# RWKV-7 chunk scan in a hybrid attention layer: the prompt as a third lane beside the sample's two directions, Gram products on quarters of the array

## The chip, the cores and the metric

The kernel runs on one core of one Trainium2 chip. The metric is the device time of one execution in microseconds (us), lower is better. The engines named below are PE (TensorE, matrix products), DVE (VectorE), ACT (ScalarE), POOL (GpSimd) and SP, the queue that issues every DMA of this kernel.

## The reference

One layer of a hybrid backbone is computed for 512 sample tokens and 128 prompt tokens (width 2048). A shared input projection feeds eight attention heads and sixteen RWKV-7 heads of 64; their outputs are joined, projected, normalised, and followed by a SwiGLU feed-forward part. What the change touches is the RWKV scan: for each of 16 heads a 64x64 state S is carried along the tokens, once forward and once backward. The sample's scans start from given states, the prompt's scans start from zero, and the prompt's final states are outputs.

```python
def step(S, inp):
    r_t, w_t, k_t, v_t, kk_t, a_t = inp
    sa = jnp.einsum("bhvk,bhk->bhv", S, -kk_t)
    S = S * w_t[:, :, None, :] + sa[..., None] * (kk_t * a_t)[:, :, None, :] + v_t[..., None] * k_t[:, :, None, :]
    return S, jnp.einsum("bhvk,bhk->bhv", S, r_t)
...
for w0, w_up, a0, a_up, s0, rev in directions:
    s_fin, y_dir = _wkv_scan(s0, r_h, heads(decay), k_dir, v_h, kk, heads(a), rev)
    ys.append(y_dir)
y = ys[0] + ys[1]
```

## The kernel before

The tokens lie along the free axis, 640 columns (512 sample, then 128 prompt); features lie on the 128 partitions. The program has two stages. In the first, several jobs share PE: the input projection (`main`), the modulation weights (`wmods`), the RWKV scan (`rwkv`) and, when `main` has ended, the attention (`attention`). Each job is a generator that yields the time for which it expects to wait; a planner (`Jobs`) keeps a model of PE's time (`Tensor.now`), always takes the ready job of lowest rank (RWKV is rank 0, the projection 4, the attention 3) and so writes down one fixed order of PE's instructions. The waits it reckons with are constants in a table (`HOP`). The other engines' queues are ordered by the framework's scheduler. The second stage (output projection and feed-forward part, tile names `b`, `qh`, `mx`) begins when the first has ended and is not touched.

The scan is worked in chunks of 64 tokens, ten chunks for 640 tokens, for two heads at a time (a pair, one head on each half of the partitions): 8 pairs, each in two passes j = 0, 1. In a pass the columns are two halves of 320: half j is walked forward (d = 0), the other half backward (d = 1, its columns reversed by `view`). So each pass has two lanes of five chunks, chunk e of lane d being number 5d + e; a second pass continues from the carried states `cy`. The prompt's two chunks stand at the end of the forward order, and its states start from zero inside the lane (table `AFTER`).

A pass goes like this:
- `rwkv_decays` and `rwkv_prep` make `nk` (two key-like factors of 64 rows per head) and `pr` (two query-like factors).
- `rwkv_grams` forms for each chunk and head h the 128x128 Gram product of `nk` and `pr`: stationary `nk` with 64 rows and 128 columns, moving `pr` with 128 columns, so one half of the array's rows per head; the heads go to two PSUM banks. Four chunks fill the banks; ACT copies out `mab` and `mrb`, DVE masks the rest into `pr`. At the end DVE masks `mrb` in one go.
- `inverse` inverts the triangular `mab` (DVE, and packed 32x32 products on PE). Beside it run `rwkv_turned` (turns the values `v` into `sv` and `zv` and `nk` into `bk`, on PE) and a side job: `beside_first` (normalisation and gate of the pair before, `rwkv_post`, then the decays of the second pass) or `beside_second` (bonus term, then the next pair's load and decays).
- `rwkv_chain` walks the five steps. A step is: px = pr x sv (4 products), copied to `xs` by ACT; the products of the outputs of the step before (`outputs`, 8 products in two banks); psg = u x xs (4), copied to `zv` by ACT (head 0) and DVE (head 1); pn = bk x zv (4), and four scalar_tensor_tensor on DVE that write the next state into `sv`. POOL prepares the decayed state `sd`. After psg and after pn the planner may put other jobs' work.

PSUM tiles of the RWKV part are named `m` (three banks); those of the projection `acc`; of the modulation weights and the attention's values `x`. All matrix work of the projection and the scores uses the whole 128x128 array. Helper lines: L115 matmul, L119 transpose, L229 tensor_tensor, L238 scalar_tensor_tensor, L241 activation; L878 copies `xs`, L899 and L900 copy `zv`, L816 and L820 copy `mab` and `mrb`, L956 stores the pair's result, L1245 stores an attention head, L847 loads the states, L448 stores the shifted r, k, v.

Of the kernel before, what the change touches and what calls it, by code (L numbers as in the profile page):

```python
# [11 lines left out]
ALU = mybir.AluOpType  # L12
# [3 lines left out]
P = 128  # L16
# [30 lines left out]
for _n, _w in (("ident", 128), ("gmask", 128), ("lmask", 32), ("par", 2), ("blk", 128), ("cen", 128), ("blk2", 2), ("sel", 2),  # L47
               ("ones", 1), ("rst", 320), ("rot", 128)):
    CST[_n] = (_off, _w)
    _off += _w  # L50
# [110 lines left out]
def step_kernel(ctx: ExitStack, tc: tile.TileContext, a: dict, o: dict, upto: int = 99, npairs: int = NPAIR, dbg=None):  # L161
# [32 lines left out]

    def half(name):
        return rtile(name, HN, "h", 1)
# [210 lines left out]
    def token_shift(p0, p1, mi, mk=edge):  # L407
# [12 lines left out]
        return ((slice(0, NS), s[:, :NS]), (slice(NS, NT), s[:, 513:641]))  # L420
# [260 lines left out]
    def nat(d, j):  # L681

        h = j if d == 0 else 1 - j
        return slice(h * HN, h * HN + HN)

    def view(t, d, j):
        v = t[:, nat(d, j)]
        return v if d == 0 else v[:, ::-1]
# [25 lines left out]
    HV = [slice(0, HN), slice(HN, NT)]  # L714

    def rwkv_decays(i, j, sh):
# [3 lines left out]
        for d in range(2):  # L720
# [3 lines left out]
            for t, w, x, r_, b, ps in both:  # L724
                T.matmul(ps[:, :HN], w, x[:, nat(d, j)], start=True, stop=False)

            for t, w, x, r_, b, ps in both:
                T.matmul(ps[:, :HN], w[r_], xl[r_, nat(d, j)], start=False, stop=True, share=0.5)
            for t, w, x, r_, b, ps in both:
                od = t[:, HV[d]] if d == 0 else t[:, HV[d]][:, ::-1]  # L730
                act(od, ps[:, :HN], AF.Tanh, bias=b[:, col: col + 1], scale=0.5)
            yield 2 * HOP["dec"]
        ts(V, ld, ld, -0.5 * EXPH, -0.5 * EXPH)
        for v_ in HV:
            V.tensor_tensor_scan(out=ld[:, v_], data0=con("rst"), data1=ld[:, v_], initial=0.0, op0=ALU.mult, op1=ALU.add)
# [6 lines left out]
        for d in range(2):  # L742
            stt(nb[:, HV[d]], ta[:, HV[d]], 1.0, view(kk, d, j), ALU.add, ALU.mult)
        ts(V, ta, ta, ka_h[:, i: i + 1], ka_c[:, i: i + 1])
        for d in range(2):
            tt(V, ta[:, HV[d]], ta[:, HV[d]], view(k, d, j), ALU.mult)
        for d in range(2):
            n_ = ks[:, nat(d, j)]
            src = ta[:, HV[d]] if d == 0 else ta[:, HV[d]][:, ::-1]
# [6 lines left out]
    def rwkv_prep(i, j, sh, u):  # L756
# [5 lines left out]
        for h in range(2):  # L762
# [3 lines left out]
            for d in range(2):  # L766
                es = slice(5 * d, 5 * d + 5)
                kv_, rv_ = (ch(t[rh, nat(d, j)]) for t in (kk, r))
                if d == 1:
# [3 lines left out]
                tt(G, pr[h][rh, es, 1, :], rv_, dd5[rh, es, :], ALU.mult)  # L773
        yield HOP["prep"] + (FIRST[1] if i + j == 0 else 0.0)

    def rwkv_turned(i, j, sh, u):

        nk, v = u["nk"], sh["v"]
# [1288 lines left out]
```

## Time and profile before

| | |
|---|---|
| runs (3) | median 3418.34 us, 3415.4 to 3426.62 |
| profiled execution | 3418.1 us, its instructions span 3416.3 us |
| first stage | 0 to 1434 us |
| RWKV passes | first chain about 260 us, last result stored at 1428.9 us |
| attention heads stored | 1155.1 to 1433.0 us |
| mean granted PE clock | 0.969 |

A row of the profile names the engine, the operation, the tile written and the tiles read, then the shape. PE writes two records for a float32 product and one for a product of rounded operands. In a row of PE, `64*128` is the part of the array in use (rows*columns). A burst of equal products is merged into one row of the timeline with its count; the time from its start to the next row's start is what it takes of PE's time, since records overlap.

### The profile page before, as it was taken

What the parts mean: (1) busy time and instruction counts of PE and PEld (TensorE: products, weight loads), DVE (VectorE), ACT (ScalarE), POOL (GpSimd) and SP (SyncE); (2) the same over time, 40 slices, a digit from 0 to 9 for tenths busy, and PEclk for the clock granted to TensorE, in tenths of its full rate; (3) what the DMA queues carried; (4) which work ended last, traced back from release to release, by engine and by line L of the source; (5) the groups of instructions that cost most, each with busy time, mean ns of one, the idle gap of its engine ahead of it and who ended that gap; (6) DMA issues with size and microseconds to landing.
All of it is one profiled execution on the core that took longest, in us unless ns stands there. A gap on an engine that the chain in (4) does not pass through costs nothing.

```text
span 3416.3 us, 71056 instructions
## 1 busy us (share of the span) xinstructions
PE 3231.4 (95%) x27746; PEld 2973.9 (87%) x27746; DVE 2489.4 (73%) x4469; ACT 1447.3 (42%) x3028; POOL 994.2 (29%) x1034
## 2 busy tenths in 40 slices
PE   7999998999997988899989999999999999999998
PEld 3777777777876777799989999999999999999997
DVE  2466675666658666568688888888887769999677
ACT  1344343444444545445454444444444444333234
POOL 0012222222222222112265444444442332222124
PEclk9999998999998999999989999999999999999998
DMA  9755454542222110275434443344444367888643
GB/s 359 241 185 166 145 171 142 158 151 94 66 63 84 44 34 28 79 246 173 145 108 154 149 139 124 127 141 135 130 123 121 114 218 278 298 286 285 214 142 119
DMA packets 289344, 527.71 MB, mean 154 GB/s; under 512 B 30512, under 2 KB 76272, under 8 KB 289008
## 3 DMA queue, kind: packets, MB, share of 16 engines
q1 hardware_dynamic: 289008, 523.18, 46.7%
q8 instruction: 217, 3.56, 0.4%
q14 instruction: 119, 0.97, 0.1%
HBM read 428.99 MB, written 92.44 MB: 153 GB/s over the span
## 4 chain that ended last, share of the span: by engine, by line
PE 65%; DVE 8%; ACT 3%; issue 2%; DMA 2%; POOL 2%; SPq 0%; ACTq 0%; DVEq 0%; POOLq 0%
PE b L115 51%; PE acc L115 7%; PE m L115 5%; PE x L115 1%; DVE ql L229 1%; DVE pr L229 1%; POOL z L229 1%; DVE z L229 1%; DVE ip L229 1%; ACT z L241 0%; DMA z<-zd 0%; PE acc L119 0%; DMA k<-rkv 0%; DVE nk L238 0%; DVE wlo L229 0%
## 5 line engine op out<-in xcount | busy, mean ns | idle before, releaser
L229 DVE TENSOR_TENSOR ql<-raw,qh 128x512 fp32r<-128x512 f32 (+1 forms) x1064 | 888.6, 850 | 264.9 <-ACT qh L1307 250.6
L1307 ACT CAST qh<-raw 128x512 fp32r<-128x512 f32 (+1 forms) x1064 | 633.5, 610 | 831.0 <-PE b L115 643.2
L115 PE MATMUL b<-t,qh 128*128 128x320 f32 x2816 | 623.4, 310 | 8.3 <-ACT qh L1307 7.1
L229 POOL TENSOR_TENSOR raw<-raw,raw 128x512 f32<-128x512 f32 x240 | 351.8, 1466 | 807.1 <-DVE ql L229 561.2
L115 PE MATMUL b<-op,qh 128*128 128x320 f32 x2560 | 552.8, 311 | 2.0 <-DMA op<-hd 1.2
L115 PEld LDWEIGHTS b<-t,qh 128*128 128x128 f32 x2816 | 473.1, 189 | 9.6 <-ACT qh L1307 8.1
L115 PE MATMUL b<-p,qh 128*128 128x320 f32 x2112 | 469.5, 311 | 0.0
L115 PE MATMUL b<-t,ql 128*128 128x320 f32 x1408 | 436.2, 311 | 5.4 <-DVE ql L229 5.4
L115 PEld LDWEIGHTS b<-op,qh 128*128 128x128 f32 x2560 | 425.8, 189 | 4.0 <-ACT qh L1307 1.9
L115 PE MATMUL b<-op,ql 128*128 128x320 f32 x1280 | 378.9, 311 | 5.6 <-DVE ql L229 5.5
L115 PEld LDWEIGHTS b<-p,qh 128*128 128x128 f32 x2112 | 356.9, 190 | 0.1
L115 PE MATMUL b<-p,ql 128*128 128x320 f32 x1056 | 329.4, 312 | 6.1 <-DVE ql L229 6.1
L115 PE MATMUL acc<-xh,whi 128*128 128x320 f32 x1056 | 265.2, 333 | 9.7 <-ACT P L1170 3.9
L115 PEld LDWEIGHTS b<-t,ql 128*128 128x128 f32 x1408 | 265.3, 189 | 7.3 <-DVE ql L229 7.3
L115 PE MATMUL acc<-xh,wlo 128*128 128x320 f32 x1056 | 264.6, 333 | 4.8 <-DVE wlo L229 4.8
L115 PE MATMUL acc<-xl,whi 128*128 128x320 f32 x1056 | 261.5, 330 | 0.5 <-DVE xl L229 0.5
L115 PEld LDWEIGHTS b<-op,ql 128*128 128x128 f32 x1280 | 236.7, 189 | 8.4 <-DVE ql L229 8.2
L115 PE MATMUL b<-mh,qh 128*128 128x320 f32 x1024 | 230.2, 314 | 7.0 <-ACT qh L1307 6.0
L115 PEld LDWEIGHTS acc<-xh,whi 128*128 128x128 f32 x1056 | 180.8, 197 | 33.5 <-issue 12.7
L115 PEld LDWEIGHTS b<-p,ql 128*128 128x128 f32 x1056 | 200.1, 190 | 8.5 <-DVE ql L229 8.5
L229 DVE TENSOR_TENSOR wlo<-raw,whi 128x512 fp32r<-128x512 f32 (+1 forms) x161 | 110.3, 686 | 124.0 <-ACT whi L266 115.4
L115 PEld LDWEIGHTS acc<-xh,wlo 128*128 128x128 f32 x1056 | 180.6, 196 | 22.6 <-issue 9.2
(330 smaller groups left out, 5465.1 us busy)
## 6 DMA issues: line engine op xcount, KB each, us to landing
wm<-in_w_mod_dram SPq DMA_DIRECT2D x64, 1024.0 KB, 5.4
raw<-in_w_gate_dram SPq DMA_DIRECT2D x188, 256.0 KB, 2.7
raw<-in_w_up_dram SPq DMA_DIRECT2D x188, 256.0 KB, 2.9
op<-hd SPq DMA_DIRECT2D x136, 320.0 KB, 5.3
wm<-in_w_mod_dram SPq DMA_DIRECT2D x64, 512.0 KB, 7.5
raw<-in_w_out_dram SPq DMA_DIRECT2D x128, 256.0 KB, 2.9
raw<-in_w_down_dram SPq DMA_DIRECT2D x128, 256.0 KB, 5.4
raw<-in_w_in_dram SPq DMA_DIRECT2D x127, 256.0 KB, 2.7
```

The costliest lines, as they stand in the source:

```text
L115: self.eng.matmul(out, lhsT, rhs, start=start, stop=stop)
L229: eng.tensor_tensor(out=out, in0=x, in1=y, op=op)
L1307: A.copy(hi, x)
```

## The change

The columns of the RWKV part are kept in another order: 256 of the sample, the 128 of the prompt, the other 256 of the sample. A pass now has a segment of six chunks (columns 0 to 384) and one of four. In pass j the segment g is walked forward where g = j, backward otherwise. The six-chunk segment holds a lane of four chunks and, as a third lane, the prompt's two chunks, whose states start from zero at once. So a chain has four steps: two of three lanes and two of two lanes, ten chunks in all as before. The products of `outputs` for all lanes go to one PSUM bank instead of two.

The Gram product of a chunk and head is split into two products of 64 columns of `nk` each, four per chunk, each on its own quarter (64x64) of the array; the quarters that give `mab` and `mrb` of both heads now share one bank, so ACT copies `mab` for both heads at once, and DVE masks `mrb` straight out of PSUM, per group of four chunks. The turned values (`sv`, `zv`), until now made by `rwkv_turned`, are made inside `rwkv_grams`, after the second and the third group of chunks; the reversed copy `vr` is made at the end of `rwkv_prep`. `rwkv_turned` sets the start states (until now done by the chain) and makes `bk`. The shifted columns are stored with three DMAs instead of two, the pair's result with three instead of one. The decays' products are 384 and 256 columns wide instead of 320 and 320. A scratch area for DMAs is set to 1024 bytes; no constant of `HOP` is changed.

```diff
-        return ((slice(0, NS), s[:, :NS]), (slice(NS, NT), s[:, 513:641]))
+        return ((slice(0, 256), s[:, :256]), (slice(256, 384), s[:, 513:641]), (slice(384, NT), s[:, 256:NS]))
...
+    SEG = (slice(0, 384), slice(384, NT))
+    CHS = (slice(0, 6), slice(6, NCH))
...
     def rwkv_turned(i, j, sh, u):
-        nk, v = u["nk"], sh["v"]
-        vr = half("vr")
-        A.copy(vr, view(v, 1, j))
-        sv_, zv, bk = u["sv"], u["zv"], u["bk"] = wide("sv"), wide("zv"), wide("bk")
-        yield HOP["vr"]
-        for d in range(2):
-            src = v[:, nat(0, j)] if d == 0 else vr
-            es = slice(5 * d, 5 * d + 5)
-            ps = mps()
-            for c in range(5):
-                for h in range(2):
-                    T.matmul(ps[hrow(h), cc(c)], src[rows(h), cc(c)], ident[rows(h), rows(h)], start=True, stop=True)
-            for h in range(2):
-                A.copy(sv_[hrow(h), es, h, :], ch(ps[hrow(h), :HN]))
-                A.copy(zv[hrow(h), es, h, :], ch(ps[hrow(h), :HN]))
-            yield HOP["tv"]
+        nk, cy = u["nk"], sh["carry"]
+        sv_, bk = u["sv"], u["bk"]
+        for h in range(2):
+            if j == 0:
+                for d, q in ((0, 0), (1, 6)):
+                    DMA.dma_start(out=sv_[rows(h), q, h, :], in_=a["states"][d, i, rows(h)])
+                G.memset(sv_[rows(h), 4, h, :], 0.0)
+            else:
+                G.tensor_copy(sv_[rows(h), 2:7:4, h, :], cy[rows(h)].rearrange("p (d v) -> p d v", v=C))
+                G.memset(sv_[rows(h), 0, h, :], 0.0)
+        yield 0.4
...
-        for e0, n in EG:
+        for n_, (e0, n) in enumerate(EG):
             es = slice(e0, e0 + n)
             both = [mps(), mps()]
             for e in range(n):
-                for h, ps in enumerate(both):
-                    T.matmul(ps[:, e * P: e * P + P], nk[rows(h), e0 + e].rearrange("p b t -> p (b t)"),
-                             pr[h][rows(h), e0 + e].rearrange("p b t -> p (b t)"), start=True, stop=True, share=0.5)
-            for h, ps in enumerate(both):
-                ps4 = ps[:, :n * P].rearrange("p (c b t) -> p c b t", b=2, t=C)
-                q = 1 - h
-                A.copy(mab[rows(h), es], ps4[rows(h), :, 0, :])
-                tt(V, pr[h][rows(q), es].rearrange("p c b t -> p c (b t)"),
-                   ps4[rows(q)].rearrange("p c b t -> p c (b t)"),
-                   con("gmask")[rows(q)].unsqueeze(1).broadcast_to([C, n, P]), ALU.mult)
-                A.copy(mrb[rows(h), es], ps4[rows(h), :, 1, :])
+                for h in range(2):
+                    for b in range(2):
+                        T.matmul(both[b != h][rows(b), e * P: e * P + P], nk[rows(h), e0 + e, b, :],
+                                 pr[h][rows(h), e0 + e].rearrange("p b t -> p (b t)"), start=True, stop=True, share=0.33)
+            pa, pb = (ps[:, :n * P].rearrange("p (c b t) -> p c b t", b=2, t=C) for ps in both)
+            A.copy(mab[:, es], pa[:, :, 0, :])
+            for h in range(2):
+                q = rows(1 - h)
+                tt(V, pr[h][q, es].rearrange("p c b t -> p c (b t)"), pb[q].rearrange("p c b t -> p c (b t)"),
+                   con("gmask")[q].unsqueeze(1).broadcast_to([C, n, P]), ALU.mult)
+            tt(V, mrb[:, es], pa[:, :, 1, :], con("gmask")[:, C:].unsqueeze(1).broadcast_to([P, n, C]), ALU.mult)
+            if n_:
+                values(n_ - 1)
             yield 2 * HOP["gram"]
-        tt(V, mrb, mrb, con("gmask")[:, C:].unsqueeze(1).broadcast_to([P, NCH, C]), ALU.mult)
...
-        for e in range(5):
+        for e in range(4):
+            qs_ = lanes(e)
             px = mps()
-            for d in range(2):
+            for l, q in enumerate(qs_):
                 for h in range(2):
-                    T.matmul(px[rows(h), cc(d)], pr[h][:, 5 * d + e, 0, :], sv_[:, 5 * d + e, h, :], start=True, stop=True)
+                    T.matmul(px[rows(h), cc(l)], pr[h][:, q, 0, :], sv_[:, q, h, :], start=True, stop=True)
...
-            A.copy(lanes(zv, 0, e), lane2(psg, 0))
-            V.tensor_copy(lanes(zv, 1, e), lane2(psg, 1))
+            A.copy(both(zv, 0, e), lane2(psg, 0))
+            V.tensor_copy(both(zv, 1, e), lane2(psg, 1))
+            if len(qs_) > 2:
+                A.copy(zv[rows(0), qs_[2], 0, :], psg[rows(0), cc(2)])
+                V.tensor_copy(zv[rows(1), qs_[2], 1, :], psg[rows(1), cc(2)])
             yield HOP["s"]
...
-                for d in ds:
-                    q = 5 * d + e
...
-                    stt(dst, pn[rh, cc(d)], dc[rh, q: q + 1], sd[rh, cc(d)], ALU.mult, ALU.add)
+                for l in ls:
+                    dst = place(l, e)
+                    dst = dst[rh, h, :] if len(dst.shape) > 2 else dst[rh]
+                    stt(dst, pn[rh, cc(l)], dc[rh, qs_[l]: qs_[l] + 1], sd[rh, cc(l)], ALU.mult, ALU.add)
...
-        DMA.dma_start(out=mix_d[8 + i], in_=y)
+        for out, src in ((slice(0, 256), slice(0, 256)), (slice(256, NS), slice(384, NT)), (slice(NS, NT), slice(256, 384))):
+            DMA.dma_start(out=mix_d[8 + i][:, out], in_=y[:, src])
```

How PE's order changes is shown at two places. The first is the chain in the first pass of the third pair (`sv`, `pr`, `zv`, `bk`, `mrb`, `uf` are the chain's tiles, `acc` the projection's): a step of the chain before,

```order
L115 MATMUL m_6363<-xs_6346,uf_162 64x64 x4
L115 MATMUL acc_6070<-xh_922,wlo_6168 128x320 x2
L115 MATMUL acc_6070<-xh_931,whi_6167 128x320 x2
L115 MATMUL acc_6070<-xl_932,whi_6167 128x320 x2
L115 MATMUL acc_6070<-xh_931,wlo_6168 128x320 x2
L115 MATMUL m_6378<-zv_5778,bk_5779 64x64 x4
L115 MATMUL acc_6070<-xh_1184,whi_6266 128x320 x2
L115 MATMUL acc_6070<-xl_1185,whi_6266 128x320 x2
L115 MATMUL acc_6070<-xh_1184,wlo_6267 128x320 x2
L115 MATMUL m_6399<-sv_5777,pr_5542 64x64
```

and a step of three lanes in the changed kernel:

```order
L115 MATMUL m_6316<-xs_6293,uf_162 64x64 x6
L115 MATMUL acc_6163<-xl_634,whi_6164 128x320 x2
L115 MATMUL acc_6163<-xh_633,wlo_6165 128x320 x2
L115 MATMUL acc_6163<-xh_642,whi_6164 128x320 x2
L115 MATMUL acc_6163<-xl_643,whi_6164 128x320 x2
L115 MATMUL m_6335<-zv_5591,bk_5592 64x64 x6
L115 MATMUL acc_6163<-xh_642,wlo_6165 128x320 x2
L115 MATMUL acc_6163<-xh_651,whi_6164 128x320 x2
L115 MATMUL acc_6163<-xl_652,whi_6164 128x320 x2
L115 MATMUL m_6354<-sv_5590,pr_5556 64x64
```

The same amount of the projection's work stands between the bursts of a step; the bursts are longer, and a chain has four steps of them instead of five.

The second place is the turning of the values (`v`, `vr` against the identity in `cst`) in the next pass, the second of that pair. Before, the two bursts stand by themselves after the Gram products (`ks` and `wm` belong to other jobs):

```order
L115 MATMUL m_6710<-ks_5020,cst 128x320
L115 MATMUL m_6713<-cst,v_4911 64x64 x10
L115 MATMUL x_6611<-wm_1111_6612,cs 32x512 x4
L115 MATMUL m_6749<-cst,vr_6689 64x64 x10
L115 MATMUL acc_6524<-xl_932,whi_6577 128x320 x2
```

In the changed kernel each follows a group of Gram products (`pr`, `nk`; here the third and last group):

```order
L115 MATMUL m_6645<-pr_6471,nk_6470 64x128
L115 MATMUL m_6646<-pr_6471,nk_6470 64x128
L115 MATMUL m_6646<-pr_6472,nk_6470 64x128
L115 MATMUL m_6645<-pr_6472,nk_6470 64x128
L115 MATMUL m_6645<-pr_6471,nk_6470 64x128
L115 MATMUL m_6646<-pr_6471,nk_6470 64x128
L115 MATMUL m_6646<-pr_6472,nk_6470 64x128
L115 MATMUL m_6645<-pr_6472,nk_6470 64x128
L115 MATMUL m_6659<-cst,v_4960 64x64 x8
L115 MATMUL acc_6626<-xh_422,whi_6536 128x320 x2
```

The transposes of `v` and `vr` have moved into the Gram bursts, ahead of the inverse. On ACT the group's evictions, before this row set (one of the three groups),

```order
L816 COPY mab_6490<-m_6551 64x256
L816 COPY mab_6490<-m_6552 64x256
L266 CAST whi_6577<-raw_6529 128x512
L820 COPY mrb_6491<-m_6551 64x256
L820 COPY mrb_6491<-m_6552 64x256
```

become one copy followed by those of the values:

```order
L820 COPY mab_6512<-m_6564 128x256
L808 COPY sv_6509<-m_6586 64x6x64
L809 COPY zv_6510<-m_6586 64x6x64
L808 COPY sv_6509<-m_6586 64x6x64
L809 COPY zv_6510<-m_6586 64x6x64
```

Three of ACT's four copies of a group are gone from its queue; the values' copies, which stood behind the inverse's start, now stand ahead of it.

On DVE, the second step of a chain, with three lanes (a later pair; `y` the outputs, `zv` and `sv` as above, `fs` the prompt's final state) look like this; before, a step has one copy of `zv` and four scalar_tensor_tensor:

```order
L226 TENSOR_TENSOR y_9858<-m_10859,y_9858 128x64 x3
L913 COPY zv_10155<-m_10875 64x2x64
L916 COPY zv_10155<-m_10875 64x64
L235 SCALAR_TENSOR_TENSOR sv_10154<-m_10894,dc_9745,sd_10854 64x64 x2
L235 SCALAR_TENSOR_TENSOR fs_9857<-m_10894,dc_9745,sd_10854 64x64
L235 SCALAR_TENSOR_TENSOR sv_10154<-m_10894,dc_9745,sd_10854 64x64 x2
L235 SCALAR_TENSOR_TENSOR fs_9857<-m_10894,dc_9745,sd_10854 64x64
```

A three-lane step has six of these updates and two copies where a step before had four and one.

More of the change, by code (lines that the diff above doesn't have):

```diff
@@ L841, in rwkv_chain @@
+        gap = first[1] - first[0]
         if j == 0:
@@ L843, in rwkv_chain @@
             sh["y"] = slot("y")
-        for h in range(2):
-            if j == 0:
-                for d, e in ((0, 0), (1, 7)):
-                    DMA.dma_start(out=sv_[rows(h), e, h, :], in_=a["states"][d, i, rows(h)])
-                G.memset(sv_[rows(h), 5, h, :], 0.0)
-            else:
-                G.tensor_copy(lanes(sv_, h, 0), lane2(cy, h))
-                G.memset(sv_[rows(h), 3, h, :], 0.0)
-        y = sh["y"]
-        def outputs(c):
-            pss = [mps()[:, :C] for _ in range(2)]
-            ms = (slice(0, C), slice(None, None, -1))
-            for d, ps in enumerate(pss):
+        y, fs = sh["y"], sh["fs"]
@@ new lines, in lanes, with both, lane2, place @@
+        def lanes(e):
+            return [q + e for q in first] + ([(4, 0)[j] + e] if e < 2 else [])
+        def both(t, h, e):
+            return t[rows(h), first[0] + e: first[1] + e + 1: gap, h, :]
+        def lane2(t, h):
+            return t[rows(h), :2 * C].rearrange("p (d v) -> p d v", v=C)
+        def place(l, e):
+            if l == 2:
+                return sv_[:, lanes(e)[2] + 1] if e == 0 else fs[:, cc(j)]
+            if e < 3:
+                return sv_[:, lanes(e)[l] + 1]
+            return cy[:, cc(1 - l)] if j == 0 else None
@@ L860, in outputs @@
+        def outputs(e):
+            qs_ = lanes(e)
+            ps = mps()
+            turned = [(q >= 6) != j for q in qs_]
+            for l, q in enumerate(qs_):
                 for h in range(2):
-                    T.matmul(ps[rows(h)], sv_[:, 5 * d + c, h, :], pr[h][:, 5 * d + c, 1, :][:, ms[d]], start=True, stop=False)
-            for d, ps in enumerate(pss):
+                    T.matmul(ps[rows(h), cc(l)], sv_[:, q, h, :], pr[h][:, q, 1, :][:, ::-1 if turned[l] else 1],
+                             start=l == 0, stop=False)
+            for l, q in enumerate(qs_):
@@ L863, in outputs @@
                 for h in range(2):
-                    T.matmul(ps[rows(h)], zv[rows(h), 5 * d + c, h, :], mrb[rows(h), 5 * d + c, :][:, ms[d]], start=False, stop=True)
-            for d in range(2):
-                yc = y[:, nat(d, j)][:, cc(c if d == 0 else 4 - c)]
+                    T.matmul(ps[rows(h), cc(l)], zv[rows(h), q, h, :], mrb[rows(h), q, :][:, ::-1 if turned[l] else 1],
+                             start=False, stop=l == len(qs_) - 1)
+            for l, q in enumerate(qs_):
+                c = q if not turned[l] else 15 - q if q >= 6 else 5 - q
+                yc = y[:, cc(c)]
```

124 lines of the change are left out of this document (65 added, 59 removed).

## The prediction

> **What bounds the kernel now.** I read the page's busy shares first, then the table by stage, the waits of PE, and the timeline of PE inside one chain. The page:
>
> ```profile
> PE 3231.4 (95%) x27746; PEld 2973.9 (87%) x27746; DVE 2489.4 (73%) x4469; ACT 1447.3 (42%) x3028; POOL 994.2 (29%) x1034
> ```
>
> PE is nearly always busy. By stage (start, end and length in us, then busy time and count of PE, PEld, DVE, ACT and POOL, then the granted PE clock):
>
> ```profile
> 200.00:1060.00 860.00, 800.77 (x9820) 656.77 (x9819) 560.01 (x1230) 365.90 (x927) 190.53 (x324) 0.96 0.41 131
> 1060.00:1434.00 374.00, 328.26 (x3856) 285.60 (x3856) 251.92 (x581) 177.99 (x450) 93.75 (x141) 0.94 0.11 34
> ```
>
> The change lies in these 1234 us, of which PE is busy 1129; 105 us are idle. The clock costs more: 860 x 0.04 + 374 x 0.06 = 57 us. The two belong together:
>
> ```profile
> 936.00:939.00 3.00, 0.95 (x15) 0.96 (x14) 2.02 (x4) 0.00 (x0) 2.83 (x5) 1.00 0.55 151
> 939.50:942.90 3.40, 3.40 (x15) 3.40 (x14) 2.80 (x4) 1.65 (x4) 0.00 (x0) 0.50 0.27 96
> ```
>
> A gap of 2 us is followed by 3.4 us at half clock, so it costs nearly 4. Who is waited for (idle us, times, longest):
>
> ```profile
> PE m L115 <- DVE y L229: 22.1, 19, 2.7
> PE m L115 <- DVE zv L900: 6.5, 4, 4.1
> PE m L115 <- POOL sv L851: 6.0, 6, 1.2
> PE x L115 <- DMA wm<-in_w_mod_dram: 1.1, 1, 1.1
> ```
>
> No single wait is large, and hardly any is on a DMA. RWKV and attention, which fill PE together, end together (the stores of their results; min/median/max duration in ns, first and last start):
>
> ```profile
> L956 SPq DMA_DIRECT2D mix<-y x8: 319/326/327, 389.4 to 1428.9; - x8
> L1245 SPq DMA_DIRECT2D mix<-att x8: 320/326/327, 1155.1 to 1433.0; - x8
> ```
>
> So the stage ends when PE's work is done, not when the chain's latency allows. A shorter chain is worth only what it takes off PE. What PE pays per step shows in the timeline (start, length, then the burst):
>
> ```profile
> 917.54 0.49 PE L115 MATMUL m<-sv,pr 128*64 128x64 f32 x8
> ...
> 919.51 0.46 PE L115 MATMUL acc<-xh,wlo 128*128 128x320 f32 x2
> 919.80 0.45 PE L115 MATMUL acc<-xh,whi 128*128 128x320 f32 x2
> 920.19 0.45 PE L115 MATMUL m<-zv,bk 128*64 128x64 f32 x8
> 920.57 0.56 PE L115 MATMUL acc<-xl,whi 128*128 128x320 f32 x2
> 920.97 0.46 PE L115 MATMUL acc<-xh,wlo 128*128 128x320 f32 x2
> 921.26 0.45 PE L115 MATMUL acc<-xh,whi 128*128 128x320 f32 x2
> 921.65 0.49 PE L115 MATMUL m<-sv,pr 128*64 128x64 f32 x8
> 921.93 0.44 PE L115 MATMUL m<-pr,sv 128*64 128x64 f32 x8
> 922.30 0.45 PE L115 MATMUL m<-mrb,zv 64*64 64x64 f32 x8
> ```
>
> A step takes 921.65 - 917.54 = 4.11 us. Two projection products take 0.29 us (919.51 to 919.80); just ahead of a burst on a part of the array they take 0.39, and just behind one 0.40. The changes of the array's division have a price of their own.
>
> **The change part by part.** First, the bursts. More rows on them, of the values' products, the Gram groups, the inverse and the attention's values:
>
> ```profile
> 886.81 0.80 PE L115 MATMUL m<-cst,v 64*64 64x64 f32 x20 [0.82 <-DVE rms_s L229]
> 887.54 0.56 PE L115 MATMUL acc<-xl,whi 128*128 128x320 f32 x2
> ...
> 899.05 0.89 PE L115 MATMUL m<-tc,mab 32*32 32x32 f32 x80
> 899.86 0.42 PE L115 MATMUL m<-xw,lw 128*128 128x320 f32 x1
> ...
> 944.07 1.16 PE L115 MATMUL m<-pr,nk 64*128 64x128 f32 x16
> 945.16 0.56 PE L115 MATMUL acc<-xl,whi 128*128 128x320 f32 x2
> ...
> 948.59 0.71 PE L115 MATMUL m<-pr,nk 64*128 64x128 f32 x8
> 949.24 0.42 PE L115 MATMUL acc<-xh,whi 128*128 128x320 f32 x1
> ...
> 1337.84 1.27 PE L115 MATMUL x<-PT,vS 128*128 128x128 f32 x10
> 1339.04 0.28 PE L115 MATMUL m<-zv,bk 128*64 128x64 f32 x2
> ```
>
> A burst of 8 records of 64 columns takes 0.38 us (920.19 to 920.57), one of 20 takes 0.73: 0.029 per record, and 0.15 fixed. With 0.10 ahead and 0.11 behind, one excursion from whole-array work costs 0.36 us besides its records. Counted in PE's order, up to the second stage, the kernel leaves whole-array work 395 times before and 327 times after: two bursts less for the missing step of each of 16 passes, two for the turned values that now ride on Gram bursts. 68 x 0.36 = **24.5 us less**. Inside a step, going over from 128*64 to 64*64 costs 0.09 (0.37 from 921.93 against 0.28 from 921.65), with 16 fewer: **1.4 less**. The number of the chain's products is the same, ten chunks per pass; so are the decays' columns (384 + 256 for 320 + 320).
>
> Second, the Gram products. Now 8 records of 128 columns more take 1.09 - 0.65 = 0.44 us, 0.055 each, while a whole-array record of 128 columns takes 0.12 (10 in 1.20): the two halves work at once. Quarters: the values' records of 64 columns at 0.029, half of their 0.06 alone, show two at once; the inverse's of 32 columns, (0.81 - 0.25) / 80 = 0.007 against 0.03 alone, show four at once. A chunk has 4 records now, 0.22 us, and 8 after. Four at once gives 8 x 0.028 = 0.22, no change; two at once gives 0.44, and 160 chunks x 0.22 = 35 us more. Below zero nothing, since four quarters are the whole array. I take **0**, by the inverse's row, the only one with four tiles, and keep 35 for the range. The Trainium skill (TensorE: Matmul & The Clock Gate, Measured speedup vs the span model) gives 3.07 times for four tiles; by that, an estimate, a chunk would take 0.29 us and the sum come out about 10 us higher. The inverse's row, four times, decides for me.
>
> Third, the waits inside the chain:
>
> ```profile
> 919.23 0.29 DVE L900 COPY zv<-m 64x128 f32<-64x128 f32 x1
> 920.76 0.99 DVE L238 SCALAR_TENSOR_TENSOR sv<-m,dc,sd 64x64 f32<-64x64 f32 x4 [1.24 <-PE m L115]
> ...
> L899 ACT COPY zv<-m 64x128 f32<-64x128 f32 x70 | 18.2, 259 | 31.7 <-PE m L115 30.8
> ```
>
> The four updates end at 921.75, and the products that need them start at 921.65: there is no spare. With three lanes there are six, at 0.25 each: 0.50 us later after the first step, and 0.25 after the second, where the fifth update is the last that is needed. 16 x 0.75 = 12 us, if nothing covers it. The longer bursts of outputs (8 records more, 0.23 us, in each of two steps) cover part of the other wait, for `xs`; I take **6 more**, the range 0 to 12. The copies of `zv` end at 919.52 and pn starts at 920.19, 0.67 later; the second pair of copies costs 0.26 on ACT and 0.29 on DVE, if in turn 0.55, which just fits: nothing. If DVE is late, 0.55 x 2 x 16 = 18 more. POOL's two extra `sd` products per three-lane step have that whole step to hide in.
>
> Fourth, Gram's waits and evictions:
>
> ```profile
> L115 PE MATMUL m<-pr,nk 64*128 64x128 f32 x520 | 45.4, 293 | 11.4 <-DVE y L229 5.8 <-POOL sv L851 5.0 <-ACT mrb L820 0.4
> L115 PE MATMUL m<-xa,lw 128*128 128x320 f32 x26 | 9.6, 368 | 12.4 <-DVE y L229 11.7 <-DVE kk L238 0.7
> L820 ACT COPY mrb<-m 64x256 f32<-64x256 f32 x52 | 19.1, 367 | 10.4 <-DVE pr L229 9.7
> L229 DVE TENSOR_TENSOR pr<-m,cst 64x512 f32<-64x512 f32 x52 | 35.8, 689 | 32.1 <-ACT mab L816 31.0
> L229 DVE TENSOR_TENSOR mrb<-mrb,cst 128x640 f32<-128x640 f32 x13 | 10.3, 793 | 0.0
> ```
>
> Of the 22.1 us waited for `y`, 11.7 belong to the decays behind `rwkv_post`, which are not touched. Gram's 5.8 (a bank still held by the last outputs) can go, since outputs hold one bank instead of two; but Gram waits for prep's products on POOL and DVE as well, so I take **3 less**, range 0 to 5.8. On ACT nine copies of about 0.37 per pass go; ACT is 42% busy and off the path: nothing. On DVE the masking of `mrb` in three pieces out of PSUM costs between one 0.79 and three 0.69; that is under 1.3 us per pass ahead of the inverse, covered by the projection's and the attention's work that the planner puts into its wait of 12 us: nothing. If that filler is gone, it shows as a wait on `tc`.
>
> Fifth, SP: 43 more DMAs (25 shifted columns, 2 of the low-rank input, 16 results) at 0.33 us each are 14 us of its queue in 1234; the states' loads go ahead of the inverse. PE waited 1.1 us for DMAs: nothing. The result's three DMAs have the rest of the stage.
>
> Sixth, the tail. In the new order 25 of the attention's 32 value blocks stand ahead of RWKV's last product, against 30 before. Seven run with no RWKV work between, and there the scaling shows:
>
> ```profile
> L235 POOL TENSOR_SCALAR P<-P,smx 128x640 f32<-128x640 f32 x32 | 25.7, 804 | 164.7 <-DVE smx L1171 121.5 <-DVE it L590 21.6 <-PE acc L119 11.5
> ```
>
> Between 0 and 7 x 0.80 = 5.6; **3 more**.
>
> Sum: -24.5 - 1.4 + 0 + 6 - 3 + 3 = -20 us, from the profiled execution's 3418.1 (span 3416.3), which is 0.2 under the median 3418.34. That gives **3398 us**.
>
> **The rivals.** (1) The quarters work only two at a time: the Gram groups take 35 us more, 3433 us, slower. It decides from 0.35 us per chunk on (0.22 + 20/160). For it: no row has four tiles of 64x64. Against it: the inverse's fours. The Trainium skill speaks for it (TensorEngine Tiling (Array Packing), Gotcha 1: PSUM Pressure): different row tiles, it says, cannot access one PSUM bank at the same time, and here two quarters of different rows share each bank. By that rule the trace's values' products, which put both row halves into one bank, would not run two at once; at 0.029 us they do. (2) The three-lane waits are uncovered: 12 + 18 for the 6, 3422 us. For it: the step has no spare; against it: DVE loses its waits for `mab` (31.0 us). (3) The chain's latency is the bound after all: 16 x 4.11 = 66 us less, 3352. Against it: 91% of the stage is PE work. (4) Gaps close besides, since ACT and DVE are freer: a tenth of the 105 us idle and of the 57 lost to the clock is 16, and Gram's and the decays' waits for `y` make it 20: 3378 us.
>
> **How the numbers follow.** Forecast 0.55, (1) 0.13, (2) 0.12, (3) 0.06, (4) 0.14. A measurement of this kernel tells about 0.3%, 10 us, from no change. The forecast's own range is 3386 to 3412, which is the unknown of the chain's waits and of where gaps fall: 0.45 of its 0.55 is faster, 0.10 the same. (2) is the same in 0.08 and slower in 0.04, (1) slower, (3) and (4) faster: 0.65, 0.18 and 0.17. The range goes from 3372, below (4), to 3434, at (1); it leaves out (3) and the upper part of (1).
>
> **What would show it.** Right: the stage ends near 1414; Gram groups of 32 records of 64*64 take about 1.1 us with the switch; PE rows of `sv,pr` after a three-lane step wait some tenths for DVE `sv`; no Gram wait on `y`. Wrong: groups of 1.9 us or more (rival 1), more idle on `zv` and `sv` than 15 us (rival 2), or a new gap with half clock at each pass.

## The result and the profile after

| | before | after |
|---|---|---|
| median of the runs | 3416.87 us (4) | 3377.47 us (4; 3373.67 to 3383.53) |
| ratio | | 0.9884 [0.9856, 0.9912] |
| span of the profiled execution | 3416.3 us | 3371.9 us |
| mean granted PE clock | 0.969 | 0.975 |
| records of PE that leave whole-array work, first stage from 200 us | 358 | 291 |

The change takes about 40 us off, twice the 20 of the forecast. 3377 lies in the widest range that was given (3372 to 3434), but below the forecast's own (3386 to 3412); it is the number of rival 4 (3378), which had a chance of 0.14. The page of the changed kernel, busy time by engine:

```profile
PE 3193.5 (95%) x28386; PEld 2952.9 (88%) x28386; DVE 2489.2 (74%) x4520; ACT 1400.1 (42%) x2890; POOL 1010.7 (30%) x1050
```

PE works 38 us less than before, ACT 47 less; DVE the same. The end of the first stage is best read at the first product of the second (`b<-mh,qh`), which comes at 1438.0 us before and at 1391.9 after. The table by stage from 200 us to there (start, end, length; busy time of PE, PEld, DVE, ACT and POOL; PE clock), before:

```profile
200.00:1438.00 1238.00, 1129.05 (x13677) 942.39 (x13676) 812.46 (x1812) 545.03 (x1379) 284.27 (x465) 0.95 0.32 102
```

and after:

```profile
200.00:1391.90 1191.90, 1096.49 (x14359) 927.79 (x14357) 818.62 (x1867) 499.67 (x1243) 303.04 (x484) 0.97 0.34 107
```

The stage is 46.1 us shorter; the rest of the program takes 1978.3 and 1980.0. Of the 46.1, idle time of PE (length less busy time) gives 108.9 - 95.4 = 13.5. The busy time falls by 32.6, and part of that is the clock: PE stands at half clock for 126 us of the stage before and for 82 after. Half of such time, where PE was busy, is lost: 53.7 us before, 34.9 after, 18.8 less. What is left, the products at full clock, goes from 1075.4 to 1061.6, 13.8 less. So in these two traces about a third of the gain is work that PE no longer does, and two thirds are gaps and time at half clock. (The two profiled executions differ by 44 us, the medians by 39.) The forecast's sum had -26 for the work, +6 net for waits and the tail, and nothing for gaps in other jobs or for the clock.

Gaps and half clock belong together. In the first stages of all fourteen traces below, 152 of the 174 gaps of PE of 2 us or more are followed by a stretch at half clock within 3.5 us, 65 of the 124 from 1.5 to 2 us, and 98 of the 1102 shorter ones.

The stores of the two jobs that share PE (min/median/max ns, first and last start):

```profile
L978 SPq DMA_DIRECT2D mix<-y x24: 319/384/882, 386.1 to 1362.6; - x24
L1267 SPq DMA_DIRECT2D mix<-att x8: 319/327/332, 1132.3 to 1386.9; - x8
```

RWKV now ends 66 us earlier (1428.9 before), attention 46 (1433.0 before): the last 24 us are attention alone.

### The profile page after: what moved, and what is told of

Read it like the earlier page. It is cut to its first block, busy times and chain, and to the rows that moved or that the text cites. A ratio compares the mean times of both kernels' runs of the same rounds, so it can differ in the third digit from the quotient of the medians.

```text
span 3371.9 us, 72309 instructions
## 1 busy us (share of the span) xinstructions
PE 3193.5 (95%) x28386; PEld 2952.9 (88%) x28386; DVE 2489.2 (74%) x4520; ACT 1400.1 (42%) x2890; POOL 1010.7 (30%) x1050
## 4 chain that ended last, share of the span: by engine, by line
PE 59%; DVE 6%; ACT 2%; issue 2%; DMA 1%; POOL 1%; SPq 0%; ACTq 0%; DVEq 0%; POOLq 0%
PE b L115 52%; PE acc L115 4%; PE m L115 3%; DVE z L226 1%; DVE ql L226 1%; PE x L115 1%; POOL z L226 1%; ACT z L238 0%; PE acc L119 0%; DMA qt<-qr 0%; DVE pr L226 0%; DVE smx L1191 0%; ACT P L1192 0%; DVE wlo L226 0%; DVE z L235 0%
## 5 line engine op out<-in xcount | busy, mean ns | idle before, releaser
L115 PE MATMUL acc<-xh,wlo 128*128 128x320 f32 x1056 | 255.0, 323 | 2.7 <-DVE wlo L226 2.6
L263 ACT CAST whi<-raw 128x512 fp32r<-128x512 f32 (+1 forms) x161 | 95.7, 595 | 240.8 <-PE acc L115 200.3
```

What stands on the lines that cost most here:

```text
L115: self.eng.matmul(out, lhsT, rhs, start=start, stop=stop)
L263: A.copy(hi, r)
```

## The experiments

Four theories stood against each other. **A**: the gain is the price of an excursion from whole-array work, 0.36 us by the prediction's rows (0.3 in the last expectations), and what comes besides has another cause. **B**: it comes from the Gram part, whose evictions and banks changed. **C**: it comes from the shorter chain, four steps on three lanes. **D**: it is the luck of one order of the program, which happens to have fewer gaps. Later came **I**: the parts act only together.

All kernels were decomposed as above (the idle time is the stage's length less PE's busy time; loss is half the busy time at half clock; work is the rest). An excursion is a record that leaves whole-array work. There is one trace of each kernel; the ratio is that of all its runs to those of the kernel before on the same chip:

| kernel | excursions | work | idle | loss | idle + loss | stage end | ratio to before |
|---|---|---|---|---|---|---|---|
| before | 358 | 1075.4 | 108.9 | 53.7 | 162.6 | 1438.0 | 1 |
| before_jit | 352 | 1077.5 | 107.3 | 65.1 | 172.4 | 1450.0 | 1.0050 [1.0032, 1.0068] |
| gram_only | 319 | 1063.0 | 118.8 | 46.6 | 165.4 | 1428.4 | 1.0008 [0.9998, 1.0017] |
| gram_jit | 320 | 1066.7 | 125.6 | 59.0 | 184.6 | 1451.3 | 1.0061 [1.0040, 1.0082] |
| lanes_only | 328 | 1075.0 | 100.5 | 62.0 | 162.5 | 1437.5 | 0.9975 [0.9961, 0.9989] |
| lanes_jit | 319 | 1072.0 | 88.6 | 38.0 | 126.6 | 1398.6 | 0.9904 [0.9887, 0.9920] |
| split_values | 323 | 1072.2 | 103.3 | 34.2 | 137.5 | 1409.7 | 0.9946 [0.9928, 0.9965] |
| after | 291 | 1061.6 | 95.4 | 34.9 | 130.3 | 1391.9 | 0.9884 [0.9856, 0.9912] |
| after_same | 292 | 1065.0 | 95.5 | 31.2 | 126.7 | 1391.6 | 0.9882 [0.9866, 0.9899] |
| after_jit | 295 | 1060.2 | 94.2 | 35.0 | 129.2 | 1389.3 | 0.9889 [0.9873, 0.9906] |
| evict_old | 291 | 1063.8 | 106.5 | 36.5 | 143.0 | 1406.9 | 0.9936 [0.9918, 0.9955] |
| lane_major | 291 | 1075.0 | 100.4 | 35.6 | 136.0 | 1411.0 | 0.9937 [0.9914, 0.9959] |
| after_gup1_5 | 292 | 1062.2 | 89.6 | 34.9 | 124.5 | 1386.7 | 0.9881 [0.9864, 0.9899] |
| after_gup2_5 | 286 | 1058.8 | 99.8 | 39.3 | 139.1 | 1397.8 | 0.9913 [0.9899, 0.9928] |

How far one row can be trusted: `after` and `after_same` are the same program, and their work differs by 3.4 us and their loss by 3.7. The profiled execution of `before` took 3418.1 us, where the kernel before has medians of 3410 to 3413 on the three chips of these experiments; that of `lanes_only` took 3414.57, the slowest of its ten, at their lowest clock (0.966), 13 us over its median. The loss and the stage end of these two rows are high by some such amount.

**Each part alone.** `gram_only` keeps two lanes of five steps and takes the quartered Gram products, their evictions and the values turned in Gram bursts:

```diff
-                for h, ps in enumerate(both):
-                    T.matmul(ps[:, e * P: e * P + P], nk[rows(h), e0 + e]...
+                for h in range(2):
+                    for b in range(2):
+                        T.matmul(both[b != h][rows(b), e * P: e * P + P], nk[rows(h), e0 + e, b, :], ...
...
+            if n_:
+                values(n_ - 1)
```

> Two lanes and five steps as before, but Gram products on quarters, one copy of mab, mrb masked out of PSUM, and the values turned inside the Gram bursts. 355 excursions. Theory A: 40 x 0.36 = 14 less and 3 for the bank: 3400. Theory B (evictions and banks give the surplus): 3380. Theory C (the chain gives it): 3400.

Measured: 3412.80 us against 3410.58, no change, where all three theories had a gain. Work fell by 12.4 us in its trace, and idle time took 9.9 of that back; its loss is 7.1 lower, but against a trace of `before` that lies 8 us over that kernel's median here. `lanes_only` takes the three lanes and the new order of columns, with the Gram halves, their evictions and the values' own bursts as they were:

```diff
-        for e in range(5):
+        for e in range(4):
+            qs_ = lanes(e)
...
+        vr = rtile("vr", 384, "h", 1)
...
+        yield HOP["vr"]
+        for g in (j, 1 - j):
...
+            yield HOP["tv"]
```

> Three lanes and four steps, but Gram products on halves and the values turned in bursts of their own, as before. PE leaves whole-array work 364 times (395 before, 327 with the whole change). Theory A, the price of an excursion (0.36 us each): 31 x 0.36 = 11 less, with 6 to 9 more for waits of three lanes and the tail, 3408 to 3412 when before is 3417. Theory B, the surplus of the change (40 us gained where 20 were reckoned) comes from the evictions and banks of the Gram part: no surplus here, the same 3410. Theory C, the surplus comes from the shorter chain: 3385 to 3395.

Measured: 3401.61 against 3410.58, 9 us faster, where the whole change gives 38 to 40: what theories A and B had forecast, and not C. So neither half alone carried the gain, and their sum was 30 us short of it. But one gap of its trace stands out. The timeline of PE, then the table of the gap and of what follows it:

```profile
1095.00 1.29 PE L115 MATMUL m<-tc,mab 32*32 32x32 f32 x80 [12.08 <-DVE tc L602]
```

```profile
1083.00:1095.00 12.00, 0.00 (x0) 0.03 (x1) 11.70 (x18) 2.16 (x4) 1.07 (x3) 0.59 0.30 87
1095.00:1098.40 3.40, 3.40 (x131) 2.57 (x135) 0.49 (x1) 0.46 (x1) 0.00 (x0) 0.50 0.07 14
```

For 12 us PE does nothing while DVE is busy for 11.70: 6.2 us of that on the attention's operands (`araw`, `xl`, `cl`), which stand between the inverse's own steps (5.6 us), the last of which writes `tc`. Then PE runs at half clock for 3.4 us more. No other of the fourteen traces has a gap of over 10 us in this stage. It looked like an accident of the order, and it called for a second order of each part (below).

**The same kernel again, and the values taken out of the Gram bursts.** `after_same` is the changed kernel once more, beside the others on one chip. `split_values` adds one line, after which the planner may put other work between a Gram group and the values' products:

```diff
             if n_:
+                yield 0.3
                 values(n_ - 1)
```

> The changed kernel once more, for a second trace of it beside the others on one chip. All theories: 3377, give or take 5. If idle time and half-clock time of PE in the first stage (95 and 85 us in the first trace, 109 and 130 before) repeat within some 5 us, they belong to the order; if they scatter by 20, they are chance of the single execution.

> The changed kernel, with a planner's wait of 0.3 us between each Gram group and the values behind it, so that these are bursts of their own again: 359 excursions for 327. Theory A: 32 x 0.36 = 11 us more than the changed kernel, 3389. Rival, the bursts' merging costs nothing because other work filled the drain: same as the changed kernel, 3377.

Measured: 3372.54 us for the first, with the same stage end within 0.3 us and the same idle time within 0.1: in this pair the gaps belong to the program, not to the execution. The second took 3395.70: 32 more excursions in the trace, 23 us more time, twice what theory A had and far from the rival's nothing. Work rose from 1061.6 to 1072.2, 0.33 us an excursion (0.23 if `after_same`, with 1065.0, is the base); 7.9 us more idle time and the clock's -0.7 make it 17.8, by which the two stages differ. The other 5 us lie between the medians and the traces.

**Another order of the same program.** `before_jit` and `after_jit` change one constant of the planner that has nothing to do with the change, the time it expects between two chunks of the modulation weights:

```diff
-         "wm": 5.98, "ev": 1.0, "sq": 3.77},
+         "wm": 5.6, "ev": 1.0, "sq": 3.77},
```

> The kernel before with one planner's constant moved (the wait for a modulation weight block, 5.98 to 5.6), which does nothing but shuffle PE's order: 390 excursions for 395. Theory D, the 20 us by which the change beat its reckoning (idle and half-clock time of PE, 163 us before, 127 to 130 after, 162 and 165 with either part alone) are luck of one order: this kernel moves by 10 us or more either way. Theory A, they come from the change: within 5 us of before.

> The changed kernel with the same constant moved: 336 excursions for 327. Theory D (luck of one order): it loses much of the surplus, 10 to 25 us slower than the changed kernel, idle and half-clock time back near 150. Theory A (the change itself): 3 us slower for the excursions, no more.

Measured: 3429.54 and 3373.66 us where the kernel before takes 3412.62. The kernel before lost 17 us; the stages of the two traces differ by 12.0, of which 11.4 are clock loss. The changed one stood where it was. So here an order's luck is worth up to 17 us, but the gain is not one lucky order: against its own second order it is 56 us.

**Same order of PE, other work beside it.** `evict_old` (nine more copies on ACT in a pass, 144 in all; the 18 of the expectation are those of a pair) gives the changed kernel the old evictions: four copies on ACT per group and one masking of `mrb` at the end:

```diff
-            A.copy(mab[:, es], pa[:, :, 0, :])
+            for h in range(2):
+                A.copy(mab[rows(h), es], pa[rows(h), :, 0, :])
+                A.copy(mrb[rows(h), es], pa[rows(h), :, 1, :])
...
-            tt(V, mrb[:, es], pa[:, :, 1, :], con("gmask")...
...
+        tt(V, mrb, mrb, con("gmask")...
```

> The changed kernel with the evictions of before: per group two copies each of mab and mrb on ACT, 18 copies of 0.26 to 0.37 us more per pass half of them on the path to the inverse, and mrb masked at the end. PE's order is the same to the instruction. Theory B (freed ACT and banks give the surplus): 10 to 20 us slower than the changed kernel. Theory A: 0 to 5 slower. Theory D says nothing, since the order stays.

Measured: 3390.79 us, 17 to 18 more than the changed kernel; in the traces 15, of which 11.1 are idle time (106.5 against 95.4) and 2.2 work. The prediction had put these evictions at nothing, since ACT is busy 42% of the time. Idle time ahead of the inverse's products, the first of which need `mab`, went from 6.6 to 14.1 us. That late copies are the cause is likely but not shown: the scheduler also put DVE's queue in another order in many places, and `lane_major` (next), with the new evictions, has 13.1 us there too.

`lane_major` lets DVE write the new states lane by lane instead of head by head; nothing else differs on PE:

```diff
-            for h in range(2):
-                rh = rows(h)
-                for l in ls:
+            for l in ls:
+                for h in range(2):
+                    rh = rows(h)
```

> The changed kernel with DVE's six state updates put lane by lane instead of head by head, so that the two that the next product needs come first. PE's order is the same. By the reckoning of the chain's waits (0.5 us after the first step and 0.25 after the second, in 16 passes) at most 12 us less, and about 4 if half of it is covered. Rival, the waits are covered already: the same time.

Measured: 3389.78 us, 16 to 18 slower, where up to 12 less had been expected, with 13.4 us more work at the same number of excursions. The timeline shows why. After, the six updates and the burst that waits for them (start, length):

```profile
958.55 1.39 DVE L235 SCALAR_TENSOR_TENSOR sv<-m,dc,sd 64x64 f32<-64x64 f32 x6 [0.49 <-PE m L115]
959.45 0.81 PE L115 MATMUL m<-sv,pr 128*64 128x64 f32 x11
```

and in `lane_major`, the same step:

```profile
966.87 1.86 DVE L235 SCALAR_TENSOR_TENSOR sv<-m,dc,sd 64x64 f32<-64x64 f32 x6 [0.49 <-PE m L115]
967.77 1.28 PE L115 MATMUL m<-sv,pr 128*64 128x64 f32 x11
```

The same six instructions take 0.47 us longer when head 0 and head 1, which lie on different halves of the partitions, alternate; the burst of PE is stretched by 0.47 as well, and since its records overlap, none of that shows as idle time. From the start of one update to the start of the next are 0.19 to 0.21 us in the median where both are of one head, and 0.30 to 0.32 where the head changes. Over the 31 three-lane steps of each trace with six updates in a row the medians are 1.39 and 1.86, so 31 x 0.47 = 14.6 us, near the 13.4; the 25 rows of four updates take 0.23 longer each (5.8 us in all), so not all of the delay is waited for.

**A second order of each part.** The same constant as above, in the kernels with one part:

```diff
-         "wm": 5.98, "ev": 1.0, "sq": 3.77},
+         "wm": 5.6, "ev": 1.0, "sq": 3.77},
```

> The three lanes alone (old Gram halves and evictions, values turned in bursts of their own), with one planning constant moved: the time after which the planner brings the next chunk of the modulation weights, 5.98 to 5.6. 349 excursions instead of 395. Theory A (price of an excursion 0.3 us, 46 fewer = -14, three-lane waits and tail +8.5, nothing else): -5, about 3406 beside 3412 for the kernel before. Theory I (the parts of the change act together: the first stage's idle time and clock loss, 128 to 143 us in every order with both parts and 162 to 172 in every order with one or none, stay at the higher level): 3396 to 3412, and the sum of idle and loss at 155 to 172. Theory D (luck of one order: the three lanes alone had one 12 us wait that another order need not have): the wait of PE on `tc` goes, and the time is 3385 to 3395, sum of idle and loss 145 or less.

> The quartered Gram products with turned values alone, on two lanes and five steps, with the same planning constant moved from 5.98 to 5.6. 349 excursions instead of 395. Theory A (0.3 us an excursion, 46 fewer): -14, about 3398 beside 3412. Theory I (parts act together): idle time and clock loss of the first stage stay at 160 to 172 us, time 3400 to 3416. Theory D (luck): it may come out anywhere within 17 us of the first version of it (3413), and below 3396 it would take the work of the interaction away.

Measured: 3376.50 and 3430.78 us where the kernel before takes 3410.33. The three lanes alone gain 34 us in this order: the 12 us gap is gone, and idle time plus loss are 126.6, as low as with the whole change. The Gram part alone loses 20. Their tables by stage, lanes first:

```profile
200.00:1398.60 1198.60, 1109.99 (x13706) 934.53 (x13704) 816.54 (x1832) 541.88 (x1385) 310.43 (x487) 0.96 0.33 106
```

```profile
200.00:1451.30 1251.30, 1125.73 (x14320) 942.82 (x14318) 818.65 (x1843) 498.32 (x1235) 284.11 (x468) 0.95 0.31 101
```

88.6 us of PE's time are idle in the one, 125.6 in the other. Theory I, by which the three lanes alone had to stay at 155 us or more, fell; its time for the Gram part, 3416 at most, was too low by 15 us. D was right that the gap on `tc` was an accident, but the time came out 9 us under its range for the lanes and 1 us over that for the Gram part. Theory A missed both, by 30 us down and 33 up: it leaves out the idle time. The ratios of two orders each:

| ratio to before | order 5.98 | order 5.6 | mean |
|---|---|---|---|
| neither part | 1 | 1.0050 | 1.0025 |
| Gram part | 1.0008 | 1.0061 | 1.0035 |
| three lanes | 0.9975 | 0.9904 | 0.9940 |
| both | 0.9882 | 0.9889 | 0.9886 |

In the mean over both columns and over the other part, three lanes are worth 0.9913 - 1.0030 = -0.0117, 40 us, and the Gram part 0.9960 - 0.9982 = -0.0022, 7 to 8 us. The four gains behind the first mean are 9, 50, 43 and 59 us, all of one sign; those behind the second are -3, -4, 32 and 5, so the Gram part's share can't be told from nothing. Nor can a part that the two have only together, the difference of differences, -0.0064, 22 us: three of the four kernels differ by 17 to 24 us between two orders of the same program.

**The largest wait that was left.** In the changed kernel one group of products has more idle time ahead of it than any other (it belongs to the decays behind `rwkv_post`):

```profile
L115 PE MATMUL m<-xa,lw 128*128 128x384 f32 x15 | 5.8, 387 | 13.3 <-DVE y L226 13.3
```

It stands behind `m<-sg,gw`, whose bank is held until POOL's `y<-y,ks` (1.53 us) and the first of DVE's products behind it are done. Two kernels raise the planner's estimate ahead of `m<-sg,gw`:

```diff
-         ... "pow2": 3.84, "gup0": 0.0, "gup": 0.36,
+         ... "pow2": 3.84, "gup0": 1.5, "gup": 0.36,      (after_gup2_5: 2.5)
```

> The changed kernel with the planner's estimate ahead of the gate product of `rwkv_post` (`gup0`) raised from 0 to 1.5 us: the two products m<-sg,gw and with them the m<-xa,lw behind them are put later in PE's order by 3 to 8 rows. In the changed kernel m<-xa,lw waits 13.3 us in eight places for DVE's y, which waits for POOL's 1.5 us addition. If the wait is a matter of place alone: 4 to 8 us of it go and with them a part of the half-clock windows behind the longest, time -5 to -10 beside the changed kernel (3373 on a chip where the kernel before takes 3412): 3363 to 3369. Theory D (order's luck): 3366 to 3385, whatever becomes of that wait.

> The same estimate raised to 2.5 us, which covers POOL's 1.5 us addition and the first of DVE's products: m<-sg,gw and m<-xa,lw come 7 to 13 rows later than in the changed kernel. If the wait is a matter of place alone: 10 us or more of the 13.3 go, with 2 to 5 us of clock loss: 3356 to 3363 where the kernel before takes 3412. If another wait takes its place (the second half's chunk factors come later, so a wait on `pr` or `tc` grows) or by the order's luck: 3366 to 3385.

Measured: 3367.52 and 3380.41 us (ratios 0.9881 and 0.9913; the changed kernel's are 0.9884 and 0.9882). The wait is gone in both, in the first already by an estimate of 1.5, but the time, against the kernel before on the same chip, is the same in the one and some 10 us longer in the other. The first lies in the range of both theories; the second refutes the one by which place alone decides. PE's waits of the first (total, times, longest):

```profile
PE m L115 <- DVE zv L913: 16.5, 9, 2.7
...
PE m L115 <- DVE y L226: 2.6, 2, 2.2
```

against the changed kernel's:

```profile
PE m L115 <- DVE y L226: 13.7, 8, 3.7
PE m L115 <- DVE zv L913: 8.6, 5, 2.8
```

Of 11 us less on `y`, 8 came back on `zv`: idle time ahead of a step's products rose from 18.1 to 26.7 us. Neither kernel beats the changed one by more than its interval.

## Why the prediction came out as it did

**Excursions (-24.5): the size is right.** Taking the three-lane kernels, the three with the values or the Gram products apart (lanes_only, lanes_jit, split_values) have 323.3 excursions and 1073.1 us of work in the mean; the six with both parts and the same order on DVE have 291.2 and 1061.9: 0.35 us each. The two pairs of two-lane kernels (355 and 1076.5; 319.5 and 1064.9) give 0.33. Both take the quartering of the Gram products as free, and both hang on works that differ by 3.4 us between two executions of one program. With 68 fewer that is -22 to -24, where 0.36 gave 24.5. The 1.4 us for the array's change inside a step are too small to be told here.

**The Gram quarters (0): right, and rival 1 is dead.** A group of 32 records of 64x64, and one of 16, each followed by a burst on quarters, in the changed kernel's timeline:

```profile
911.49 1.10 PE L115 MATMUL m<-pr,nk 64*64 64x128 f32 x32
912.42 0.86 PE L115 MATMUL m<-cst,v 64*64 64x64 f32 x24
...
916.63 0.67 PE L115 MATMUL m<-pr,nk 64*64 64x128 f32 x16
917.13 0.63 PE L115 MATMUL m<-cst,vr 64*64 64x64 f32 x16
```

(0.93 - 0.50) / 16 = 0.027 us per record of 128 columns, against 0.055 on halves and 0.12 on the whole array: all four quarters work at once, though two of different rows write the same bank. A chunk takes 8 x 0.027 = 0.22, what it took before. The rule of the Trainium skill (TensorEngine Tiling (Array Packing), Gotcha 1: PSUM Pressure) that was rival 1 does not show here. Nor does the Trainium skill's factor 3.07 (TensorE: Matmul & The Clock Gate, Measured speedup vs the span model), which the page gives for four row tiles with K=32 and N=512, another shape; the estimate from it was 0.29 us a chunk.

**The waits inside the chain (+6): right for `sv`, too small by what was put at nothing for `zv`.** At 0.33 us an excursion, three-lane kernels do 6 to 7 us more work than two-lane ones with the same parts: the two lanes-only kernels (323.5 excursions) have 1073.5, where 1076.5 - 31.5 x 0.33 = 1066.1 was due; the six with both have 1061.9, where 1064.9 - 28.3 x 0.33 = 1055.6 was. Two waits of a three-lane step make it up, one for `zv` and one for the state updates `sv`:

```profile
888.02 0.80 PE L115 MATMUL m<-zv,bk 128*64 128x64 f32 x8
889.14 0.59 PE L115 MATMUL m<-zv,bk 128*64 128x64 f32 x4 [0.32 <-ACT zv L915]
...
890.73 0.33 PE L115 MATMUL m<-sv,pr 128*64 128x64 f32 x2
891.66 0.68 PE L115 MATMUL m<-sv,pr 128*64 128x64 f32 x9 [0.59 <-DVE sv L235]
```

The waits that do show, ahead of a step's products, add up to 18.1 us, against 18.4 before. The mark that was to speak for rival 2, 15 us on `zv` and `sv`, was set badly: before, `sv,pr` and `zv,bk` have 5.1 + 8.0 = 13.1 already, and now 6.1 + 7.3 = 13.4. What is new lies inside the bursts. With the idle time left out, the 24 records of `sv,pr` and `pr,sv` behind a first three-lane step take 1.17 us in the mean, where the quickest take 0.85, the 20 behind the second 0.95 against 0.73, the 16 of a two-lane step 0.72 against 0.61 (before, 0.68 against 0.61 in all steps). The 12 records of `zv,bk` take 0.71 against 0.50; before, eight take 0.41 against 0.38. Over all passes these are, an estimate from such means outside half-clock stretches, some 6 us more than before on `sv`, as forecast, and some 5 on `zv`, which the prediction had at nothing. So a third of rival 2's 18 us did come, out of sight of the idle times. (The two ways of counting, 6 to 7 and 11, differ by about as much as two traces of one program do. Six updates take 0.40 us longer than four, not 0.50.)

**Gram's waits (-3): the term that was too small.** The groups ahead of the Gram products, before, after, and with each part alone (busy, mean ns, idle time and its releasers):

```profile
L115 PE MATMUL m<-pr,nk 64*128 64x128 f32 x640 | 55.4, 292 | 14.0 <-DVE y L229 7.5 <-POOL sv L851 6.0 <-ACT mrb L820 0.4
```

```profile
L115 PE MATMUL m<-pr,nk 64*64 64x128 f32 x1280 | 51.0, 284 | 7.7 <-DVE pr L226 5.7 <-DVE mrb L226 2.0
```

```profile
L115 PE MATMUL m<-pr,nk 64*64 64x128 f32 x1280 | 52.4, 281 | 14.1 <-DVE y L229 7.8 <-POOL sv L853 6.2
```

```profile
L115 PE MATMUL m<-pr,nk 64*128 64x128 f32 x640 | 52.7, 289 | 7.2 <-DVE pr L226 7.1
```

The third is gram_jit, the fourth lanes_jit. `y` is gone as forecast, and POOL's `sv` too, which the prediction had left in place: L851 is the memset of the prompt's start state, which the change moves from the chain's head into `rwkv_turned`. Another wait, for `pr`, takes half of their place. In the four two-lane traces this idle time is 14.0 to 15.1 us, in the ten three-lane ones 6.2 to 9.8: 7 us, not 3, and it comes with the lanes and not with the Gram part. Of gaps of 1.5 us or more, the size that is often followed by half clock, this group has 3 to 5 in the one and none or one in the other.

**Gaps in the other jobs and the clock (no term in the sum): the step that failed.** The prediction read 105 us of idle time and 57 lost to the clock, and left both as they were but for Gram's 3. Two-lane kernels have 163 to 185 us of idle time and clock loss; nine of the ten three-lane ones have 124 to 143, the tenth 162.5 with its 12 us gap and in an execution 13 us over its median. In the means idle time goes from 115 to 97 us and loss from 56 to 38: 36 us, with 25 gaps of 1.5 us or more in the first stage for two lanes and 19 for three. After Gram's 7 us the idle time is spread: in the means the attention's, the projection's and the decays' products have about 4 us less ahead of them each, the results of the modulation 1.8 less, and a step's products 1.8 more, and single kernels scatter as widely as that.

Rival 4 had gaps closing, and its 3378 is the measured time, but the agreement is in part luck. It reckoned with 20 us, for the reason that ACT and DVE are freer; DVE is as busy as before (2489 us), and the Gram part alone, which frees ACT, has no less idle time than the kernel before. The saving comes with the three-lane part as a whole. That part also takes the outputs to one PSUM bank, sets the start states early and has decays of other widths; none of these was run apart from the four steps, so which of them closes the gaps stays open.

Nor is it rival 3, the chain's latency as the bound. RWKV's last product comes 67 us earlier, about that rival's 66, but this is chance of the order: it is 93 us earlier in lanes_jit and 25 in split_values. PE is busy for 92% of the shorter stage too, and when RWKV has ended the attention goes on.

**The tail (+3) and SP (0).** RWKV's last product stands 11 us ahead of the stage's end before and 32 after; what the longer tail costs was not measured by itself. Waits of PE for the modulation weights' DMA are 6.4 us against 1.1, with 43 more DMAs in SP's queue, where the prediction had them at nothing. That the DMAs are the cause is not shown: in lanes_jit, with the same DMAs, idle time ahead of those products is 1.6, and in gram_only, without them, 8.3.

## What to carry to other kernels

When PE is shared by jobs and a planner fills it, cost a change in three parts, not one: the products and array changes that it removes, the gaps that it opens or closes, and the half clock behind the longer gaps. Here the second and third were two thirds of the gain. An edit's worth in such a kernel is known only from two or more orders of the same program: two orders of one kernel differed by up to 25 us, and the half of this change that carries most of it looked worth 9 us in one order and 34 in the next. A wait that is cut away from a full engine may come back elsewhere: 11 us less on `y` became 8 more on `zv`.

## What the runs showed of the hardware

- In a row of state updates DVE pays for going from one half of the partitions to the other: six of 64x64 take 1.39 us with one such change and 1.86 with five, four take 0.99 and 1.23 with one and three: 0.117 us per change in both.
- Four products of 64x64 on the four quarters run at once with two of different rows in one PSUM bank: 0.027 us per record of 128 columns, against 0.055 on halves.
- Waits inside a burst of products do not show as idle time of PE: the 0.47 us of lane_major's late states are hidden in a longer row of the burst, and so are most of the new waits for `zv` and `sv` of the changed kernel. A burst's length against its count of records has to be read as well as the idle times.
